# Gate and up products of a decoder layer's FFNs: pairs of column blocks by seven block products of sums instead of eight

## The chip, the cores and the metric

One core of one Trainium2 chip runs the kernel. The metric is the device time of one execution in microseconds (us). Engines are PE (TensorE; PEld is its weight load), DVE (VectorE), ACT (ScalarE), POOL (GpSimd) and SP (SyncE, which issues most DMAs).

## The reference

One layer of a decoder for 544 tokens (a prompt of 512 and 8 x 4 sampled ones) of width 1024, in float32: a SwiGLU FFN as a half step, a token mixer (gated DeltaNet and sliding-window attention) between an input and an output projection, and a second FFN. Each sub-layer is normalised before and after it, and shift, scale and gate come from a conditioning vector through `w_ada`. The change touches the two FFNs, D_FF is 2752:

```python
def swiglu(h, w_gate, w_up, w_down):
    return (jax.nn.silu(h @ w_gate) * (h @ w_up)) @ w_down

def decoder_layer(x, c, pos, conv_buf, S0, attend, p):
    mod = jax.nn.silu(c) @ p['w_ada'] + p['b_ada']
    ...
    h = rmsnorm(x, p['ffn1_norm_pre']) * (1 + sc1) + sh1
    x = x + 0.5 * g1 * rmsnorm(swiglu(h, p['ffn1_w_gate'], p['ffn1_w_up'], p['ffn1_w_down']), p['ffn1_norm_post'])
```

## The kernel before

The modulated input lies transposed in SBUF as a pair `hh`, `hl` of a rounded high part and its remainder, each 128 x 8 x 544: eight blocks of 128 input channels, and 544 tokens in two halves of TH = 272. Weights come in units of four blocks of 128 x 128. For a unit SP issues a DMA of 256 KB (`wload`), ACT casts it to the high part `hi` (L270), and DVE, in some units POOL, subtracts for the remainder `lo` (L271). PE then multiplies three terms per block, hi by xh, hi by xl and lo by xh, each for both token halves (`mm3`, L301): 24 matmuls of N = 272 to a unit.

An FFN goes in two halves of its inner width. In each, gate and up are computed for column blocks of 128 (`up`: two units each of gate and up, K = 1024), then `finish` takes silu of gate (ACT, L607), multiplies by up (DVE, L609) and splits the result into `fh`, `fl` (L612, L616); `last` does a mixed block of 64 and 64 columns; then `down` runs over eight output blocks and adds into `d`. The first half has column blocks 0 to 10, the second 0 to 9 and the mixed one. In the second FFN the first NFRONT = 5 blocks go one token half after the other, since the first half's tokens are ready sooner.

`Feed` holds the units in order. When unit i is to run, units up to i + 1 have been split and up to i + 2 been loaded (SPLIT_AHEAD, LOAD_AHEAD); four raw buffers and three of hi and lo (RAW_BUFS, HL_BUFS) bound it. Beside the feed, side streams run: `rest` computes the ada vectors of the later sub-layers during the first FFN, with 56 loads `wa` of 512 KB, each for four matmuls `adaps` (L467). The order of each engine is fixed when the kernel is built, by a planner that takes turns by the times that the streams yield; on the chip each engine works its own list in order.

Of the kernel before, what the change touches and what calls it, by code (L numbers as in the profile page):

```python
# [38 lines left out]
RAW_BUFS = 4  # L39
HL_BUFS = 3  # L40
# [152 lines left out]
class Unit:  # L193
# [3 lines left out]
    def __init__(self, parts, go, boxes=None, pool_lo=False, keep=None):  # L197

        self.parts, self.go, self.pool_lo, self.keep = parts, go, pool_lo, keep
        self.boxes = boxes or [p[:5] for p in parts or ()]  # L200


class Feed:


    def __init__(self, L):
        self.L, self.units, self.at, self.raws, self.ws = L, [], 0, {}, {}

# [8 lines left out]
    def prep(self, i):  # L217
        if i not in self.ws:
            self.fetch(i)
            u = self.units[i]  # L220
            dest = u.keep() if u.keep else None
            self.ws[i] = self.L.wsplit(self.raws.pop(i), u.boxes, u.pool_lo, dest) if u.parts else dest

    def run(self, upto=None):
        n = len(self.units) if upto is None else upto
        while self.at < n:
            i = self.at
            last = len(self.units) - 1
            for j in range(i, min(i + SPLIT_AHEAD, last) + 1):
                self.prep(j)  # L230
# [6 lines left out]
class Layer:  # L237
# [55 lines left out]
    def mm3(self, ps, w, kt, rows, x, kx, first, last, m=P, cs=(0, 1)):  # L293
# [5 lines left out]
        for i, (a, b, r) in enumerate(terms):  # L299
            for c in cs:  # L300
# [6 lines left out]
                )  # L307

# [74 lines left out]
    def setup(self):  # L383
# [202 lines left out]

    def ffn(self, pre, x, env, front, ndown, hook, each=None):
# [11 lines left out]
        def finish(gsrc, usrc, rows, j, shift, cs):  # L599
# [16 lines left out]
            nc.vector.tensor_tensor(out=fl[:rows, j, ts], in0=hf, in1=fh[:rows, j, ts].bitcast(F32), op=ALU.subtract)  # L616

# [37 lines left out]
        def down(half, b, cs):  # L655
# [3 lines left out]
            for k0 in (0, 4, 8):  # L659
                def go(w, k0=k0):  # L660
                    if k0 == 0:
# [30 lines left out]
        for half in range(2):  # L692
# [6 lines left out]
            for j in js:  # L699
                us += up(half, j, (0, 1))  # L700
# [1268 lines left out]
```

## Time and profile before

| | us |
|---|---|
| median of 3 runs (1605.84 to 1608.16) | 1606.75 |
| the profiled execution | 1608.77 |
| its span, first to last instruction | 1607.0 |
| mean granted TensorE clock in it | 0.983 |
| PE busy | 1537.5 |
| DVE busy | 887.6 |
| ACT busy | 640.1 |
| POOL busy | 305.9 |

The rows further down come from the profiled execution. Matmuls are pipelined: one lasts some 290 ns from start to end, and the next may start long before that end, so the distance of starts is the cost of one. The granted clock is a share of full speed.

### The profile page before, as it was taken

Reading aid. Unit: us, or ns where it says so; the run is one execution under the profiler, and the core shown is the slowest. Engines: PE = TensorE matmul, PEld = TensorE weight load, DVE = VectorE, ACT = ScalarE, POOL = GpSimd, SP = SyncE. Lnnn points to the kernel's source line nnn. Section 1 sums busy time; section 2 is a strip of 40 time slices with the busy share of each in tenths; the row PEclk is TensorE's granted clock in tenths of the full one; section 3 lists DMA queues with packets and bytes.
Section 4 is the critical chain, followed back from the end, with each engine's and each line's share of the span. In section 5 each row is a group of like instructions: output and inputs, shape, how many; then the busy total and the mean of one; then the engine's idle time right before and its main releaser. Section 6 shows DMA issues by size and latency. Waiting matters only on the chain.

```text
span 1607.0 us, 33057 instructions
## 1 busy us (share of the span) xinstructions
PE 1537.5 (96%) x12851; PEld 1418.5 (88%) x12851; DVE 887.6 (55%) x2384; ACT 640.1 (40%) x1449; POOL 305.9 (19%) x443
## 2 busy tenths in 40 slices
PE   7999999999998999998999999999979999999996
PEld 4799999999977999997778888889979999999995
DVE  5433322333598787688889568665474332233365
ACT  4322222222445544445575242223556332223363
POOL 2000000000343231231122134131458000000042
PEclk9999999999999999999999899999999999999998
DMA  9554445445655334653113243624515432333353
GB/s 314 169 183 138 153 136 159 147 148 153 190 167 178 100 75 107 165 135 77 45 45 80 77 121 83 167 55 130 158 53 158 115 86 87 94 87 89 83 152 111
DMA packets 316083, 199.69 MB, mean 124 GB/s; under 512 B 37508, under 2 KB 298335, under 8 KB 315638
## 3 DMA queue, kind: packets, MB, share of 16 engines
q1 hardware_dynamic: 315638, 197.46, 43.5%
q8 instruction: 101, 1.65, 0.4%
q14 instruction: 56, 0.46, 0.1%
q0 software_dynamic: 288, 0.11, 0.0%
HBM read 182.08 MB, written 16.36 MB: 123 GB/s over the span
## 4 chain that ended last, share of the span: by engine, by line
PE 77%; DVE 13%; ACT 3%; DMA 2%; issue 2%; POOL 2%; SPq 0%; DVEq 0%; ACTq 0%; POOLq 0%
PE pg L301 16%; PE pu L301 16%; PE pb L301 16%; PE pd L301 14%; PE adaps L467 3%; DVE y L1194 2%; DVE lo L271 2%; ACT hi L270 1%; PE pov L1065 1%; DVE X L1422 1%; PE pgu L301 1%; DVE s L1016 1%; PE psc L1012 1%; PE pkq L1281 1%; DVE xT L571 1%
## 5 line engine op out<-in xcount | busy, mean ns | idle before, releaser
L270 ACT CAST hi<-raw 128x512 fp32r<-128x512 f32 (+2 forms) x502 | 287.9, 581 | 613.1 <-PE pu L301 172.1
L271 DVE TENSOR_TENSOR lo<-raw,hi 128x512 fp32r<-128x512 f32 (+2 forms) x368 | 252.9, 688 | 385.8 <-ACT hi L270 378.7
L301 PE MATMUL pb<-hh,hi 128*128 128x272 f32 (+1 forms) x1008 | 234.9, 303 | 1.4 <-ACT hi L270 0.7
L271 POOL TENSOR_TENSOR lo<-raw,hi 128x512 fp32r<-128x512 f32 (+1 forms) x104 | 140.6, 1356 | 483.1 <-ACT hi L270 460.5
L301 PE MATMUL pb<-hh,lo 128*128 128x272 f32 (+1 forms) x1008 | 227.7, 296 | 1.3 <-POOL lo L271 0.7
L301 PE MATMUL pb<-hl,hi 128*128 128x272 f32 (+1 forms) x1008 | 227.2, 295 | 1.0 <-DVE hl L271 1.0
L301 PEld LDWEIGHTS pb<-hh,hi 128*128 128x128 f32 (+1 forms) x1008 | 164.6, 191 | 12.0 <-issue 6.5
L301 PE MATMUL pd<-fh,hi 128*128 128x272 f32 x704 | 171.3, 290 | 0.0
L301 PE MATMUL pd<-fl,hi 128*128 128x272 f32 x704 | 170.2, 289 | 0.0
L301 PEld LDWEIGHTS pb<-hl,hi 128*128 128x128 f32 (+1 forms) x1008 | 165.0, 190 | 3.6 <-DVE hl L271 1.5
L301 PEld LDWEIGHTS pb<-hh,lo 128*128 128x128 f32 (+1 forms) x1008 | 164.4, 191 | 4.1 <-DVE lo L271 1.4
L301 PE MATMUL pd<-fh,lo 128*128 128x272 f32 x672 | 162.4, 289 | 4.0 <-POOL lo L271 2.2
L301 PE MATMUL pg<-hh,hi 128*128 128x272 f32 x672 | 149.6, 292 | 7.5 <-ACT hh L538 3.6
L301 PE MATMUL pu<-hh,hi 128*128 128x272 f32 x672 | 148.2, 291 | 0.0
L301 PE MATMUL pg<-hl,hi 128*128 128x272 f32 x672 | 147.0, 289 | 0.3 <-DVE hl L539 0.2
L301 PE MATMUL pu<-hl,hi 128*128 128x272 f32 x672 | 146.1, 289 | 0.0
L301 PE MATMUL pu<-hh,lo 128*128 128x272 f32 x672 | 145.3, 288 | 0.7 <-POOL lo L271 0.7
L301 PE MATMUL pg<-hh,lo 128*128 128x272 f32 x672 | 145.6, 288 | 0.0
L301 PEld LDWEIGHTS pd<-fh,hi 128*128 128x128 f32 x704 | 119.9, 188 | 8.6 <-issue 4.2
L301 PEld LDWEIGHTS pg<-hh,hi 128*128 128x128 f32 x672 | 108.8, 189 | 19.6 <-ACT hh L550 5.0
L301 PEld LDWEIGHTS pd<-fl,hi 128*128 128x128 f32 x704 | 120.2, 188 | 0.0
L301 PEld LDWEIGHTS pd<-fh,lo 128*128 128x128 f32 x672 | 114.1, 188 | 5.6 <-POOL lo L271 2.9
(469 smaller groups left out, 2628.6 us busy)
## 6 DMA issues: line engine op xcount, KB each, us to landing
raw<-w_in SPq DMA_DIRECT2D x136, 256.0 KB, 3.2
wa<-w_ada SPq DMA_DIRECT2D x56, 512.0 KB, 4.4
raw<-ffn_w_gate SPq DMA_DIRECT2D x94, 256.0 KB, 2.9
raw<-ffn_w_up SPq DMA_DIRECT2D x94, 256.0 KB, 7.0
raw<-ffn_w_down SPq DMA_DIRECT2D x92, 256.0 KB, 3.0
wb<-w_ada SPq DMA_DIRECT2D x32, 256.0 KB, 5.8
S<-state_delta SPq DMA_DIRECT2D x8, 512.0 KB, 8.0
delta_sample<-S SPq DMA_DIRECT2D x8, 512.0 KB, 3.4
```

The lines of the kernel that those rows point to most:

```text
L270: self.nc.scalar.copy(out=hi, in_=raw)
L271: (eng or self.nc.vector).tensor_tensor(out=lo, in0=raw, in1=hi.bitcast(F32), op=ALU.subtract)
L301: self.nc.tensor.matmul(out=ps[:m, c, :TH], lhsT=a[:r, kt, :m], rhs=b[:r, kx, c * TH:(c + 1) * TH], start=first and i == 0, stop=last and ...
L467: self.ada_mm = nc.tensor.matmul(out=ps[32 * j:32 * j + 32, :], lhsT=self.cT[:, k, :], rhs=was[j], start=k == 0, stop=k == 7, skip_group_c ...
L571: nc.vector.tensor_tensor(out=self.xT[:, b, s], in0=self.xT[:, b, s], in1=t[:, :n], op=ALU.add)
L1012: nc.tensor.matmul(out=ps[:, i * 256:i * 256 + nk], lhsT=self.qT[64 * h:64 * h + 64, 2 * g + i, qb * P:(qb + 1) * P], rhs=self.kd[64 * h:6 ...
L1016: nc.vector.tensor_tensor_reduce(out=s[:, i, :nk], in0=ps[:, i * 256:i * 256 + nk], in1=am[:, lo:], scale=0.125, scalar=-3e38, op0=ALU.add ...
L1065: nc.tensor.matmul(out=po[64 * h:64 * h + 64, :256], lhsT=self.vn[:, c, 64 * g:64 * g + 64], rhs=pTs[kb][:, 2 * h:2 * h + 2, :], start=kb ...
L1194: nc.vector.scalar_tensor_tensor(out=y[:, :CVN], in0=cv[:, i:i + CVN], scalar=w[i], in1=y[:, :CVN], op0=ALU.mult, op1=ALU.add)
L1281: nc.tensor.matmul(out=pv[:, j], lhsT=kq[:, n, 0, c * P:(c + 1) * P], rhs=kq[:, n, :, c * P:(c + 1) * P], start=True, stop=True)
L1422: e.tensor_tensor(out=xs, in0=xs, in1=pv, op=ALU.subtract)
```

## The change

Two adjacent column blocks of gate (or up), two halves of K and two halves of the tokens make a product of 2 x 2 by 2 x 2 blocks, with eight block products. `quad` computes it with seven (12 matmuls each, by `mm3h`): four sums S1 to S4 of weight blocks, added on POOL, and four sums T1 to T4 of token blocks, made once per FFN by `token_sums` on DVE and ACT and kept as hi and lo. `pair` makes a gate quad and an up quad; the first block of an odd number stays with `up`, the second FFN's front blocks too. So there are 5 and 5 pairs in the two halves of the first FFN, 3 and 5 in the second: 36 quads. Each of the seven weight operands of a quad is split into hi and lo; before there were four.

The products 11 and 12 go to A and B, two banks of one PSUM tile, S3 and 22 to a third, D; after each product a step of `f1` to `f7` copies or adds between PSUM and two SBUF tiles `qlo` and `qhi`. Space for the token sums comes from `osw` of the mixer and from `xT` in the first FFN: `xT` is written to DRAM (`xsq`) at the start and loaded back by `close1`, called by the first `down` of the second half, which also waits until `rest` is done. Buffers: raw 6, hi and lo 4, sums 3, T_BUFS 5, V_BUFS 3; two wk PSUM banks instead of four while quads run. Quad units are split up to two units ahead. The vectors are loaded through ACT's queue, the constants `cst` at the mixer's start.

```diff
+    def mm3h(self, out, w, x, first):
+        hi, lo = w
+        xh, xl = x
+        for k in range(4):
+            for i, (a, b) in enumerate(((hi, xh), (hi, xl), (lo, xh))):
+                self.nc.tensor.matmul(out=out, lhsT=a[:, k, :], rhs=b[:, k, :], start=first and k == 0 and i == 0,
+                                      stop=k == 3 and i == 2, skip_group_check=True)
...
+    def token_sums(self, x, tiles, tmp):
...
+        def put(i, k, t):
+            th, tl = (tiles[i][n][:, k:k + 2, :] for n in range(2))
+            nc.scalar.copy(out=th, in_=t)
+            tt(out=tl, in0=t, in1=th.bitcast(F32), op=ALU.subtract)
...
+        for k in (0, 2):
+            t1, b = new("t1"), new("tb")
+            tt(out=t1, in0=f(hh, k, 0), in1=f(hh, k, 1), op=ALU.subtract)
+            tt(out=b, in0=f(hl, k, 0), in1=f(hl, k, 1), op=ALU.subtract)
+            tt(out=t1, in0=t1, in1=b, op=ALU.add)
+            put(0, k, t1)
...
+    def quad(self, name, w, c0, x, ts, ready, tmp, after_quad, begin, low, high):
...
+        def add(n, a, b, place=None):
+            raw[n] = raw[place] if place else self.ws.tile([P, 4, P], F32, tag="sum", name="sum")
+            with self.ahead(HP_S):
+                nc.gpsimd.tensor_tensor(out=raw[n], in0=raw[a], in1=raw[b], op=ALU.add)
...
+        def f1():
+            st["lo"] = tmp.tile([P, 2, TH], F32, tag="t", name="qlo", bufs=T_BUFS)
+            nc.scalar.copy(out=st["lo"][:, 0], in_=A())
+
+        def f2():
+            nc.vector.tensor_tensor(out=st["lo"][:, 0], in0=B(), in1=st["lo"][:, 0], op=plus)
+
+        def f3():
+            st["hi"] = tmp.tile([P, 2, TH], F32, tag="t", name="qhi", bufs=T_BUFS)
+            nc.scalar.copy(out=st["hi"][:, 0], in_=A())
+
+        def f4():
+            nc.scalar.copy(out=st["hi"][:, 1], in_=D())
+
+        def f5():
+            t = st["hi"][:, 1]
+            nc.vector.scalar_tensor_tensor(out=t, in0=A(), scalar=-1.0, in1=t, op0=mul, op1=sub)
...
+        plan = (("11", lambda: xb(0, 0), A, 1, f1), ("12", lambda: xb(1, 0), B, 1, f2), ("S2", ts[1], A, 0, f3),
+                ("S3", ts[2], D, 1, f4), ("S1", ts[0], A, 0, f5), ("22", ts[3], D, 0, f6),
+                ("S4", lambda: xb(1, 1), A, 0, f7))
...
+            def go(wt, i=i, xf=xf, out=out, first=first, after=after):
+                if i == 0:
+                    begin()
+                    st["ab"] = self.pj(name)
+                while i == 2 and not ready():
+                    yield 0.5
+                if i == 3:
+                    st["d"] = self.wd(name + "d")
+                yield from self.mm3h(out(), wt, xf(), bool(first))
+                after()
...
-            for j in js:
-                us += up(half, j, (0, 1))
+            if len(js) % 2:
+                us += up(half, js.pop(0), (0, 1))
+            for n, j in enumerate(js[::2]):
+                us += pair(half, j, n > 0)
...
+    def close1():
+        L.xT = xp.tile([P, 8, T], F32, tag="xT", name="xT")
+        nc.sync.dma_start(out=L.xT, in_=xsq)
+        while "ada" not in done:
+            yield 0.5
+        L.open_pw(4)
```

In the second FFN, on PE, at the end of one unit and the start of the next, the order before was:

```order
L301 MATMUL pg_18571<-hl_91,hi_18529 128x272 x2
L301 MATMUL pg_18571<-hh_90,lo_18530 128x272 x2
L301 MATMUL pu_18602<-hh_90,hi_18565 128x272 [waits DVE_49]
L301 MATMUL pu_18602<-hh_90,hi_18565 128x272
L301 MATMUL pu_18602<-hl_91,hi_18565 128x272 x2
```

On PE in a gate quad of the second FFN (hi_18257 is product 11 into A, hi_18323 is S3 into D, hi_18277 is 12 into B) it is now:

```order
L328 MATMUL pg_18308<-hl_94,hi_18257 128x272
L328 MATMUL pg_18308<-hh_93,lo_18258 128x272
L328 MATMUL pgd_18369<-t34_15971,hi_18323 128x272 [waits Activation_49]
L328 MATMUL pgd_18369<-t34_15971,hi_18323 128x272
L328 MATMUL pgd_18369<-t34_15971,lo_18324 128x272 [waits DVE_49]
...
L328 MATMUL pg_18308<-hh_93,hi_18277 128x272 [waits Activation_49]
L328 MATMUL pg_18308<-hl_94,hi_18277 128x272
```

The two units followed each other directly; now seven matmuls of S3 stand between 11 and 12, and 12 waits for ACT, which has A to copy.

On ACT at the same places, before (sil reads the finished gate, hi are casts of later units):

```order
L612 CAST fh_17545<-fhx_18561 128x544 [waits DVE_49]
...
L270 CAST hi_18693<-raw_18661 128x512 [waits DMAHW6_49,DVE_49,PE_49]
L607 ACTIVATE sil_18687<-pg_18571 128x544 [waits PE_49]
L270 CAST hi_18724<-raw_18697 128x512 [waits DMAHW7_49,DVE_49,PE_49]
L612 CAST fh_17545<-fhx_18689 128x544 [waits DVE_49]
```

On ACT in the quad now (L684 is f1, L694 is f4, L691 is f3):

```order
L283 CAST hi_18344<-sum_18186 128x512 [waits PE_49,Activation_49]
L798 CAST fh_18024<-qlo_18178 128x544 [waits DVE_49]
L684 COPY qlo_18321<-pg_18308 128x272 [waits PE_49]
L283 CAST hi_18365<-raw_18163 128x512 [waits DMAHW6_49,PE_49,Activation_49]
L694 COPY qhi_18363<-pgd_18369 128x272 [waits PE_49]
...
L283 CAST hi_18400<-raw_18282 128x512 [waits DMAHW0_49,PE_49]
L691 COPY qhi_18363<-pg_18308 128x272 [waits PE_49]
```

The copies out of PSUM, for which PE waits, stand behind casts for later units in ACT's list.

On DVE at the start of the first FFN, where the last block of x is modulated (L551) and block 0 is finished, before:

```order
L551 TENSOR_TENSOR hl_91<-ts_531,hh_90 128x32 [waits Activation_49]
L271 TENSOR_TENSOR lo_673<-raw_640,hi_672 128x512 [waits DMAHW4_49,PE_49,Activation_49]
L609 TENSOR_TENSOR fhx_668<-pu_581,sil_666 128x544 [waits PE_49,Activation_49]
L271 TENSOR_TENSOR lo_704<-raw_676,hi_703 128x512 [waits DMAHW5_49,Activation_49]
...
L609 TENSOR_TENSOR fhx_796<-pu_709,sil_794 128x544 [waits PE_49,Activation_49]
```

On DVE at that place now (t12 holds T1 and T2, t34 holds T3 and T4; L687 is f2 of the first gate quad):

```order
L575 TENSOR_TENSOR hl_94<-ts_529,hh_93 128x32 [waits Activation_49]
L640 TENSOR_TENSOR t4_701<-t4_701,hl_94 128x544 [waits DVE_49]
L284 TENSOR_TENSOR lo_713<-sum_636,hi_712 128x512 [waits PE_49,Activation_49]
...
L687 TENSOR_TENSOR qlo_731<-pg_718,qlo_731 128x272 [waits PE_49,Activation_49]
L630 TENSOR_TENSOR t1_761<-t1_761,tb_762 128x544 [waits DVE_49]
...
L623 TENSOR_TENSOR t12_545<-t2_768,t12_545 128x544 [waits Activation_49]
...
L623 TENSOR_TENSOR t34_546<-t3_794,t34_546 128x544 [waits Activation_49]
```

The token sums have come in around the splits; the last of T2 (t12) and of T3 (t34) stand behind the end of the first quad's second product.

On SP where the first FFN's second half goes over to `down`, before:

```order
L464 DMA wa_4265<-w_ada 128x1024 [waits PE_49]
...
L279 DMA raw_4167<-ffn1_w_down 128x4x128 [waits DMAHW0_49,DVE_49]
...
L464 DMA wa_4267<-w_ada 128x1024 [waits PE_49]
L464 DMA wa_4486<-w_ada 128x1024 [waits PE_49]
L279 DMA raw_4277<-ffn1_w_down 128x4x128 [waits DMAHW7_49,DMAHW6_49,DVE_49]
```

On SP there now (xT from xsq is the load of `close1`):

```order
L488 DMA wa_4522<-w_ada 128x1024 [waits DMAHW1_49,PE_49]
...
L2017 DMA xT_4520<-xsq_89 128x4352 [waits DMAHW7_49,PE_49]
...
L488 DMA wa_4524<-w_ada 128x1024 [waits DMAHW3_49,PE_49]
L488 DMA wa_4530<-w_ada 128x1024 [waits DMAHW4_49,PE_49]
...
L488 DMA wa_4580<-w_ada 128x1024 [waits DMAHW2_49,PE_49]
L292 DMA raw_4743<-ffn1_w_down 128x2x128 [waits DVE_49]
```

The loads for the ada products stood one or two at a time among the weights; now eleven stand in a row, behind the load of xT and ahead of the next weights.

## Rows read from the trace of the kernel before

**Rows 1.** the page: busy us (share) xinstructions of each engine; the chain's share by engine

```profile
PE 1537.5 (96%) x12851; PEld 1418.5 (88%) x12851; DVE 887.6 (55%) x2384; ACT 640.1 (40%) x1449; POOL 305.9 (19%) x443
...
PE 77%; DVE 13%; ACT 3%; DMA 2%; issue 2%; POOL 2%; SPq 0%; DVEq 0%; ACTq 0%; POOLq 0%
```

**Rows 2.** stretches: us, busy of PE, PEld, DVE, ACT, POOL; clock, DMA share, GB/s

```profile
80.00:400.00 320.00, 320.00 (x2525) 300.62 (x2524) 95.33 (x152) 89.07 (x150) 0.55 (x1) 1.00 0.51 153
...
440.00:480.00 40.00, 36.87 (x267) 32.11 (x265) 35.47 (x79) 19.72 (x48) 20.12 (x20) 1.00 0.58 168
480.00:520.00 40.00, 35.94 (x254) 31.20 (x251) 33.21 (x87) 18.88 (x44) 12.63 (x20) 0.96 0.61 180
...
900.00:1240.00 340.00, 323.71 (x3000) 299.27 (x2998) 213.35 (x617) 135.68 (x325) 126.29 (x133) 0.97 0.41 112
...
1240.00:1520.00 280.00, 280.00 (x2241) 280.00 (x2241) 90.53 (x134) 87.51 (x149) 9.39 (x8) 1.00 0.34 94
```

**Rows 3.** PE one by one in the second FFN: start us, us, engine, line, operation, xcount

```profile
1303.34 0.42 PE L301 MATMUL pu<-hh,hi 128*128 128x272 f32 x2
...
1306.34 0.42 PE L301 MATMUL pg<-hh,hi 128*128 128x272 f32 x2
...
1308.84 0.41 PE L301 MATMUL pg<-hl,hi 128*128 128x272 f32 x2
...
1309.34 0.42 PE L301 MATMUL pu<-hh,hi 128*128 128x272 f32 x2
```

**Rows 4.** ACT one by one there

```profile
1309.29 0.62 ACT L270 CAST hi<-raw 128x512 fp32r<-128x512 f32 x1 [2.33 <-PE pg L301]
1309.82 0.62 ACT L607 ACTIVATE sil<-pg 128x544 f32<-128x544 f32 x1
```

**Rows 5.** DVE one by one when the first FFN's block 0 ends

```profile
59.17 0.69 DVE L271 TENSOR_TENSOR lo<-raw,hi 128x512 fp32r<-128x512 f32 x1 [2.66 <-ACT hi L270]
59.78 0.72 DVE L609 TENSOR_TENSOR fhx<-pu,sil 128x544 f32<-128x544 f32 x1
60.41 0.68 DVE L271 TENSOR_TENSOR lo<-raw,hi 128x512 fp32r<-128x512 f32 x1
```

**Rows 6.** groups by form, whole span: out<-in shapes xcount | busy us, mean ns | idle before

```profile
L1883 ACT COPY dacc<-pb 128x272 f32<-128x272 f32 x12 | 4.6, 384 | 15.1 <-PE pb L301 15.1
...
L676 DVE TENSOR_TENSOR dacc<-pd,dacc 128x272 f32<-128x272 f32 x28 | 12.3, 438 | 26.6 <-PE pd L301 26.5
...
L271 POOL TENSOR_TENSOR lo<-raw,hi 128x512 fp32r<-128x512 f32 x103 | 140.3, 1366 | 478.8 <-ACT hi L270 456.3 <-DVE rms3a L344 11.3 <-PE ppt L1051 7.9
```

**Rows 7.** DVE's remainders by form, 1240 to 1520 us, then 900 to 1240 us

```profile
L271 DVE TENSOR_TENSOR lo<-raw,hi 128x512 fp32r<-128x512 f32 x84 | 58.0, 690 | 136.9 <-ACT hi L270 136.9
...
L271 DVE TENSOR_TENSOR lo<-raw,hi 128x512 fp32r<-128x512 f32 x30 | 21.8, 727 | 19.6 <-ACT hi L270 14.5 <-PE pkt L1301 3.2 <-PE prb L353 1.7
```

**Rows 8.** PE one by one around the ada products at the first FFN's start

```profile
55.31 1.05 PE L467 MATMUL adaps<-wa,cT 128*32 128x512 f32 x4
56.29 0.39 PE L301 MATMUL pg<-hh,hi 128*128 128x272 f32 x1
56.52 0.29 PE L301 MATMUL pg<-hl,hi 128*128 128x272 f32 x1
...
60.22 0.52 PE L301 MATMUL pg<-hh,hi 128*128 128x272 f32 x2
```

**Rows 9.** stretches at the first FFN's start, columns as in Rows 2

```profile
31.00:37.00 6.00, 6.00 (x21) 2.11 (x21) 5.65 (x24) 2.83 (x9) 0.00 (x0) 0.64 1.09 358
37.00:46.50 9.50, 9.50 (x53) 4.67 (x49) 0.71 (x2) 1.20 (x2) 0.00 (x0) 1.00 0.31 89
46.50:56.50 10.00, 7.63 (x47) 5.21 (x46) 9.47 (x36) 4.93 (x13) 0.00 (x0) 1.00 0.83 270
56.50:66.00 9.50, 9.50 (x70) 8.51 (x70) 3.35 (x6) 2.92 (x5) 0.00 (x0) 1.00 0.66 223
```

**Rows 10.** DMA issues on the page: out<-in, xcount, KB each, median us to landing

```profile
wa<-w_ada SPq DMA_DIRECT2D x56, 512.0 KB, 4.4
```

More of the change, by code (lines that the diff above doesn't have):

```diff
@@ L228, in run @@
             last = len(self.units) - 1
-            for j in range(i, min(i + SPLIT_AHEAD, last) + 1):
-                self.prep(j)
+            for j in range(i, min(i + 2, last) + 1):
+                if j <= i + SPLIT_AHEAD or self.units[j].src:
+                    self.prep(j)
+            for f in self.todo.pop(i, ()):
+                f()
             for j in range(i, min(i + LOAD_AHEAD, last) + 1):
@@ L660, in go @@
                 def go(w, k0=k0):
+                    if half and b == 0 and k0 == 0:
+                        yield from env["close"]()
                     if k0 == 0:
@@ L796, in open, with take, take_small @@
         self.mp = mp
[L797 removed]
+        self.win = self.a["w_in"][0]
+    def take(self):
+        self.osw = self.qT = self.mp.tile([P, 8, T], F32, tag="osw", name="osw")
+    def take_small(self):
+        mp = self.mq = self.L.pool("mq", 1, self.ctx)
+        self.L.cst = mp.tile([P, CST["n"]], F32, name="cst")
+        self.nc.sync.dma_start(out=self.L.cst, in_=self.a["c_cst"])
         self.kqs = mp.tile([P, NH, 2, NS], F32, name="kqs")
@@ L1807, in hook1, with tsums @@
         sch.spawn(L.boundary(sqd, env["d"], 2, 3, tmp, sqx, x, c, done), c)
-    env = {"tmp": tmp, "sqd": sqd}
+    def tsums(e, ta, tb):
+        e["ready"] = False
+        e["ts"] = [(t[:, i, 0], t[:, i, 1]) for t in (ta, tb) for i in range(2)]
+        yield from L.token_sums(x, e["ts"], e["tmp"])
+        e["ready"] = True
+    def close1():
+        L.xT = xp.tile([P, 8, T], F32, tag="xT", name="xT")
+        nc.sync.dma_start(out=L.xT, in_=xsq)
+        while "ada" not in done:
+            yield 0.5
+        L.open_pw(4)
+    env = {"tmp": tmp, "sqd": sqd, "close": close1}
     m1 = feed.add(L.ffn("ffn1", x, env, 0, NDOWN, hook1))
@@ L1856, in main @@
     def main():
+        nc.sync.dma_start(out=xsq, in_=L.xT)
+        ta = mx.mp.tile([P, 2, 2, 4, TH], F32R, tag="osw", name="t12")
+        tb = xp.tile([P, 2, 2, 4, TH], F32R, tag="xT", name="t34")
+        env["ready"] = False
+        sch.spawn(tsums(env, ta, tb), 0)
+        L.open_pw(2)
         sch.spawn(rest(), 2)
         yield from feed.run(m1)
+        mx.take()
         while not ({0, "ada"} <= done):
@@ L1938, in main @@
             yield from feed.run(feed.at + 1)
+        while sch.side:
+            yield from feed.run(feed.at + 1)
+        tb = xp2.tile([P, 2, 2, 4, TH], F32R, tag="xT", name="t34")
+        assert feed.at < len(feed.units) and not feed.units[feed.at].src
+        bufs["ready"] = False
+        sch.spawn(tsums(bufs, ta, tb), 0)
         yield from feed.run()
```

153 lines of the change are left out of this document (128 added, 25 removed).

## The prediction

> **What bounds the kernel now.** I read four views, from the whole to the detail. The page's busy line says that TensorE (PE) works 96% of the span and no other engine more than 55%, and its chain of waits gives PE 77% [rows 1]. The stretches show where those shares hold: between 80 and 400 us (the first FFN) and between 1240 and 1520 us (the second) PE is busy every microsecond, at a granted clock of 1.00, which is the upper of its two levels, 2.4 GHz; DVE is busy for 30 to 32% there and ACT for 28 to 31% [rows 2]. The instructions one by one show why nothing else ends last: the weight unit that starts at 1303.34 us is followed by the next at 1306.34 and the next at 1309.34, 24 matmuls in 3.00 us, 125 ns each, without a gap [rows 3]; the next weights' cast on ACT (0.62 us) and their remainder on DVE (0.69 us) take less than half of that [rows 4, 5]. So in the stretches that the change touches the number of matmuls is the time, as long as nobody makes PE wait. Outside them PE has idle time (4.1 of 40 us between 480 and 520) [rows 2]; the change does not touch that, except at the start.
>
> **The change, part by part.**
>
> *Matmuls removed.* A pair of column blocks takes, for gate and for up, eight products of 12 matmuls before and seven now. Pairs: 5 + 5 in the first FFN, 3 + 5 in the second, 18 in all, so 18 x 2 x 12 = 432 matmuls fewer, at 125 ns [rows 3]: **54.0 us off the path**. PE stays the engine with most to do: a pair takes 168 x 0.125 = 21.0 us of it. DVE has 14 remainders, 14 other operations on 272 or 544 columns: with the rows' spacing of about 0.62 us for the wide ones [rows 5] and 0.44 us for the narrow ones [rows 6] about 13.5 us; ACT 14 casts at 0.53 us from start to start [rows 4] and 14 copies and activations, about 12 us; POOL 8 additions of 128 x 512, which the trace shows only as a subtraction, 1.37 us each [rows 6], 11 us. So the new sums hide beside PE. What is not hidden is the order in which things become ready, which follows.
>
> *Turnarounds inside a quad (seven products).* Before, a PSUM tile was filled by 48 matmuls and read once. Now A and B lie in one tile, which the order treats as one thing: after product 11 ACT copies A before 12 may start, after 12 DVE adds B before S2 may start, and so on, four handovers per quad. The scheduler puts matmuls of the third tile (D) between as cover: 7 of them at the handovers to ACT, 5 at those to DVE, as the order of the change shows.
> At an ACT handover, counted from the start of the last matmul before it: this ends after 0.29 us. The matmul before it, the last reader of the weights' high part, has ended 0.125 us sooner, and that releases the next cast, which stands ahead of the copy in ACT's order; a cast began 0.04 us after such an end (pair of 1308.84 us, over at 1309.25; cast at 1309.29 us) [rows 3, 4]. So the cast starts at 0.20, the copy 0.53 us later [rows 4] at 0.73, takes 0.38 us (the copy out of PSUM of the same 272 columns) [rows 6] and with 0.04 us to PE the product may start at 1.15. The cover lasts 8 slots of 0.125 us, 1.00. Stall: 0.15 us.
> At a DVE handover: 0.29 + 0.04 + 0.44 (an addition out of PSUM on 272 columns) [rows 6] + 0.04 = 0.81 against 6 slots, 0.75. Stall: 0.06 us; where a remainder stands ahead on DVE, up to 0.6 us more [rows 5].
> A regular quad so loses 2 x 0.15 + 2 x 0.06 = 0.42 us. About a third of the quads are not regular: the order lets the next quad's first matmuls, or D's, in as cover, and their cast and remainder are then made just in time: 0.62 and 0.69 us in a row [rows 4, 5] against a unit of 1.5 us that cannot start them earlier than its own last matmul but one; such a quad loses 0.5 to 1 us more. I take 0.7 us as the mean. Remainders lasted 690 ns while POOL was nearly idle and 727 ns where it worked 126 of 340 us [rows 2, 7]; POOL will work half of the time here, so I add 0.05. 36 x 0.75 = **27 us back on the path**. Bounds: 0, if everything comes a little sooner; above, every handover restarts PE as badly as the matmul after the ada product at 56.29 us, which took 0.39 us and let its follower start 0.23 us later instead of 0.125 [rows 8], and every DVE handover finds a remainder in front: 0.42 + 4 x 0.1 + 2 x 0.6 = 2.0 us a quad, 72 us.
>
> *Token sums at the first FFN's start.* The quads need sums of x (T1 to T4), 28 DVE operations of 128 x 544. DVE is busy for 9.47 of the 10 us up to 56.5 us with modulating x, and then for only 3.35 of 9.5 [rows 9]; that idle time is what the sums can use. But by the order DVE has 22 wide operations after the last modulation up to the end of T2, and ten more up to T3, at 0.61 to 0.63 us [rows 5]: T2 at about 56.9 + 13.9 = 71 us, T3 at 77.3. Block 0 ends at about 60.2 us [rows 8] and the products 11 and 12 take 3.0 us: PE reaches S2 at 63.2 and waits 7.8 us, then S3 (72.5) and waits 4.8: 12.6 us. Where PE has been idle for 4 of 40 us the clock read 0.96 instead of 1.00 [rows 2]; half a microsecond for that: **13 us**. Bounds 6 (T3 covered by other work) and 18. x goes to DRAM and back because the sums take its place; the way out shares the queues with the first weights at a time when the DMAs have room (89 GB/s between 37 and 46.5 us, against 358 just before) [rows 9], so nothing for it.
>
> *The burst behind the first FFN's second half.* The first down block now waits until all of the ada products are done. By the order eleven loads of 512 KB stand behind the reload of x (2.2 MB) on SP, each waits for PE to release one of three buffers, and only some hundred matmuls of `down` lie between: 2.2 + 3 x 0.5 MB at 358 GB/s [rows 9] = 10.5 us until the first three are there, of which PE's own work covers 5 us; then a load's 4.4 us landing time [rows 10] over two buffers in flight, 2.2 us, meets 2.1 us of PE work (0.25 us for each of four ada matmuls [rows 8], nine of `down`). **7 us**; bounds 0 and 18. Queued behind these on SP are the weights of the next down blocks, so they can be no earlier.
>
> *The rest at nothing.* The sums before the second FFN's quads lie under its ten front units of a token half, where DVE is free for two thirds; without that cover they would cost what they cost at the start. The vectors are loaded by ACT's queue instead of POOL's, three buffers instead of four: at most 1 us at the start. Reopening PSUM pools and the later load of constants: below what can be seen.
>
> **Sum** against the profiled execution (span 1607.0, time 1608.8 us): -54 + 27 + 13 + 7 = -7 us, 1601.8. The profiled run lies 2.0 us above the median of 1606.75, so **1600 us** for the median. What a measurement of this kernel can tell from no change is about 0.2%, 3.2 us: faster means below 1603.5, slower above 1610.
>
> **A rule beside the rows.** In the stretch 440 to 480 us PE stood for 3.1 of 40 us and the clock stayed at 1.00 [rows 2]. The Trainium skill's page "TensorE: Matmul & The Clock Gate", section "A second HAM failure mode: psum-queue depth-cycling", says that short idles between groups of matmuls that cycle through PSUM banks let the clock swing between its two levels. The trace before does not show it, and it speaks against this change; it is the fourth rival below. Likewise the page "GPSIMD Engine Reference", section "Key points", says that POOL shares its SBUF interfaces with VectorE and contends with operations of two SBUF inputs, which all the remainders are; the rows above show 37 ns of it, and the fifth rival is what it would be in full.
>
> **The rivals.**
> 1. *The handovers are covered* (faster). For it: the cover misses by no more than 0.15 us, and ada matmuls lie between in the first FFN. Against: four handovers in each of 36 quads, each within a tenth of being late. At 0.2 us a quad (7 us), 10 at the start and 5 for the burst: -32, **1575 us**. Chance 0.24.
> 2. *The handovers miss by a chain* (slower): casts and remainders are queued ahead of the PSUM reads, so each late handover also delays the next cast, and the next unit comes late too. It decides above (54 - 20) / 36 = 0.94 us a quad. At 1.5 us: 54 us, **1627 us**. For it: ACT and DVE run in order, and half the units of a quad have their weights made within two units. Against: DVE at 65% has slack for two units. Chance 0.22.
> 3. *The start and the burst cost double* (40 us instead of 20): **1620 us**. For it: both are long waits of PE behind one queue; against: bounds of 18 each. Chance 0.07.
> 4. *The clock falls in the quads.* At 0.96, as in 480 to 520 us [rows 2], 36 quads of 11.2 us lose 16 us: **1616 us**. Chance 0.05.
> 5. *The change takes away no time*, because the products are no longer PE's alone: if POOL's additions kept DVE out altogether, DVE would need 13.5 + 11 = 24.5 us a pair, 0.5 more than PE's eight products took (192 x 0.125 = 24.0): 18 x 0.5 = 9 us lost, and 20 at the start and the burst: +29, **1636 us**. Rows show remainders 5% longer instead [rows 7]. Chance 0.02.
>
> **How the numbers follow.** Forecast (1590 to 1612 around 1600): 0.40. Of it 0.26 lie below 1603.5, 0.10 within 0.2%, 0.04 above. Rival 1 is faster; the others, 0.36, slower except for 0.04 that ends near no change. Faster 0.26 + 0.24 = 0.50, same 0.14, slower 0.36. The forecast's own range is 1590 to 1612; eight in ten needs rival 1's middle and rival 2's: 1572 to 1630.
>
> **What would show it.** Right: 432 matmuls fewer on lines that read 125 ns each; PE waits named after the copies (lines 684, 691) and DVE adds (687, 698) of 0.05 to 0.3 us each, some 130 of them, 25 us in sum; one gap of 12 us between 60 and 80 us that DVE's sums end; waits for wa loads of some 7 us near 420 us; clock 1.00 in the quads. Wrong: PE without gaps in the quads (rival 1), gaps that casts or remainders end and that add up to over 34 us (rival 2), or a clock below 1.00 there (rival 4).

## The result: 1701.7 us, 5.9% slower

| | before | changed |
|---|---|---|
| median, us | 1607.45 (4 runs) | 1701.67 (4 runs, 1698.37 to 1704.33) |
| profiled execution, us | 1608.77 | 1698.37 |
| mean granted clock | 0.983 | 0.961 |

The ratio is 1.0587 (95% interval 1.0565 to 1.0608). Forecast were 1600 us, with 1590 to 1612 as the forecast's own range and 1572 to 1630 as the range for eight cases in ten.

The page of the changed kernel, the line that answers to [rows 1]: busy us, share and instructions.

```profile
PE 1557.7 (92%) x12419; PEld 1400.2 (83%) x12419; DVE 1138.4 (67%) x2674; ACT 748.2 (44%) x1699; POOL 529.0 (31%) x578
```

PE has the 432 matmuls fewer (12851 to 12419), yet it counts 20 us more as busy, since slow restarts and time at the lower clock are busy time too. POOL has 223 us more, where 144 sums at 1.37 us [rows 6] make 197; DVE has 251 us more. Where it went is read by stages. First the kernel before: gate and up, then `down`, of the first FFN's first half; the same of its second half; then, behind the mixer, the same four of the second FFN. Each stretch goes from the first matmul of a stage to that of the next; the columns are those of [rows 2].

```profile
28.80:189.40 160.60, 158.23 (x1156) 137.22 (x1157) 59.70 (x129) 48.02 (x90) 0.00 (x0) 0.98 0.55 169
189.40:262.10 72.70, 72.70 (x574) 67.74 (x573) 17.54 (x32) 18.25 (x33) 0.00 (x0) 1.00 0.49 149
262.10:399.60 137.50, 137.50 (x1087) 128.61 (x1086) 43.50 (x70) 38.90 (x65) 0.55 (x1) 1.00 0.51 152
399.60:481.20 81.60, 77.70 (x578) 68.77 (x576) 59.47 (x118) 39.78 (x92) 35.27 (x33) 1.00 0.59 173
...
1179.30:1324.30 145.00, 139.52 (x1090) 137.74 (x1091) 67.84 (x120) 66.58 (x128) 53.74 (x43) 0.99 0.42 114
...
1390.40:1516.40 126.00, 126.00 (x1011) 126.00 (x1010) 42.61 (x62) 38.32 (x64) 0.55 (x1) 1.00 0.33 89
```

The same stages of the changed kernel:

```profile
30.50:221.30 190.80, 161.18 (x1044) 130.53 (x1045) 140.50 (x228) 79.73 (x161) 62.20 (x40) 0.95 0.49 157
221.30:292.30 71.00, 71.00 (x563) 67.06 (x562) 19.28 (x29) 19.09 (x34) 8.04 (x6) 1.00 0.48 146
292.30:439.80 147.50, 137.29 (x969) 117.57 (x968) 101.47 (x138) 67.37 (x132) 53.75 (x36) 0.99 0.49 148
439.80:528.80 89.00, 82.32 (x586) 69.47 (x584) 50.09 (x116) 38.14 (x88) 35.34 (x34) 0.99 0.65 186
...
1232.50:1400.80 168.30, 145.42 (x1021) 137.53 (x1019) 130.46 (x186) 85.97 (x173) 91.42 (x66) 0.93 0.35 95
...
1466.90:1604.80 137.90, 123.66 (x891) 116.49 (x889) 97.45 (x128) 65.55 (x130) 53.23 (x36) 0.98 0.31 82
```

Each of the four gate and up stages should have become shorter, by 3.0 us a pair: 160.6 to 145.6, 137.5 to 122.5, 145.0 to 136.0, 126.0 to 111.0. They became 190.8, 147.5, 168.3 and 137.9, which is 45, 25, 32 and 27 us too long. The second FFN's second half is the cleanest: ten quads and the mixed block, 26.9 us lost, 2.7 us a quad where the forecast had 0.75. Outside the four, the stage of the burst grew by 7.4 us, and some 7 us more are spread over the rest (5.6 in the mixer, 703.7 against 698.1 us), which the forecast put at nothing; no run took these apart.

In the stage of the ten quads the table of waits names (us in total, times, longest):

```profile
PE pgd L328 <- DVE lo L284: 10.3, 6, 2.7
PE pud L328 <- DVE lo L284: 2.3, 4, 1.0
PE pg L328 <- ACT hi L283: 0.9, 2, 0.5
PE pg L328 <- DVE qlo L687: 0.7, 2, 0.4
```

PE waits for remainders on DVE, by up to 2.7 us. The table has 14.2 of the 26.9 us. (Its last row shows what one tile for A and B does: S2 goes to A, and waits for L687, which adds B.) Some 3 us are the clock: in two stretches, each behind a stop of PE of over 2 us, it read 0.50, the lower level of 1.2 GHz, and matmuls started 0.23 us apart; after other stops of that length it did not fall. The first of them:

```profile
1497.20:1500.60 3.40, 3.40 (x17) 3.40 (x16) 2.56 (x6) 1.61 (x4) 0.00 (x0) 0.50 0.27 75
```

DVE's groups say why remainders are late: `lo` of a loaded block, then `lo` of a sum, mean 786 and 1201 ns; before, 690 [rows 7]. Below them stand the product with silu (L793, two SBUF operands), and a narrow addition out of PSUM (L687), which is as long as ever.

```profile
L284 DVE TENSOR_TENSOR lo<-raw,hi 128x512 fp32r<-128x512 f32 x357 | 279.2, 786 | 174.5 <-ACT hi L283 155.3 <-PE pgd L328 5.6 <-PE pu L328 2.5
L284 DVE TENSOR_TENSOR lo<-sum,hi 128x512 fp32r<-128x512 f32 x72 | 86.5, 1201 | 13.6 <-ACT hi L283 11.5
...
L793 DVE TENSOR_TENSOR qhi<-qhi 128x544 f32<-128x544 f32 x18 | 24.8, 1380 | 0.1
...
L687 DVE TENSOR_TENSOR qlo<-pg,qlo 128x272 f32<-128x272 f32 x18 | 7.8, 436 | 10.4 <-PE pg L328 10.3
```

POOL and then DVE one by one in a quad (start us, us):

```profile
1506.77 1.29 POOL L669 TENSOR_TENSOR sum<-raw 128x512 f32<-128x512 f32 x1 [0.70 <-DMA raw<-ffn_w_gate]
1508.14 1.72 POOL L669 TENSOR_TENSOR sum<-sum,raw 128x512 f32<-128x512 f32 x1
1509.82 1.73 POOL L669 TENSOR_TENSOR raw<-raw 128x512 f32<-128x512 f32 x1
```

```profile
1508.02 0.69 DVE L284 TENSOR_TENSOR lo<-raw,hi 128x512 fp32r<-128x512 f32 x1 [1.40 <-ACT hi L283]
1508.90 1.51 DVE L284 TENSOR_TENSOR lo<-sum,hi 128x512 fp32r<-128x512 f32 x1 [0.19 <-ACT hi L283]
1511.16 0.44 DVE L687 TENSOR_TENSOR qlo<-pu,qlo 128x272 f32<-128x272 f32 x1 [0.75 <-PE pu L328]
```

The remainder of 1508.90 starts while POOL's sum of 1508.14 runs (to 1509.86) and ends 0.55 us after it, as if it had only begun then. POOL's next sum starts at 1509.82, beside the rest of that remainder, and lasts 1.73 instead of 1.29 us. The addition at 1511.16, with one operand in PSUM, runs beside POOL in its normal 0.44 us. So a remainder and a sum take turns, and the one that starts second waits. Counted over this trace, 85 remainders of 128 x 512 start while a sum runs; they last 1.47 us in the mean, and 82 of them end 0.53 to 0.56 us after the sum. The 289 that meet no operation of POOL last 0.69 us, and so do the 31 that POOL joins when they already run.

### The profile page after: what moved, and what is told of

Read it like the earlier page. It is cut to its first block, busy times and chain, and to the rows that moved or that the text cites. A ratio compares the mean times of both kernels' runs of the same rounds, so it can differ in the third digit from the quotient of the medians.

```text
span 1696.6 us, 33229 instructions
## 1 busy us (share of the span) xinstructions
PE 1557.7 (92%) x12419; PEld 1400.2 (83%) x12419; DVE 1138.4 (67%) x2674; ACT 748.2 (44%) x1699; POOL 529.0 (31%) x578
## 5 line engine op out<-in xcount | busy, mean ns | idle before, releaser
L283 ACT CAST hi<-raw 128x512 fp32r<-128x512 f32 (+3 forms) x538 | 309.4, 584 | 498.3 <-issue 143.3
L284 DVE TENSOR_TENSOR lo<-raw,hi 128x512 fp32r<-128x512 f32 (+2 forms) x404 | 302.0, 751 | 265.3 <-ACT hi L283 246.0
L314 PE MATMUL pb<-hl,hi 128*128 128x272 f32 (+1 forms) x1008 | 230.8, 298 | 1.8 <-DVE hl L284 0.9
L669 POOL TENSOR_TENSOR raw<-sum,raw 128x512 f32<-128x512 f32 x36 | 47.7, 1324 | 262.5 <-DVE lo L284 251.1
L669 POOL TENSOR_TENSOR sum<-raw 128x512 f32<-128x512 f32 x36 | 56.5, 1571 | 179.1 <-DMA raw<-ffn_w_gate 152.6
L284 DVE TENSOR_TENSOR lo<-sum,hi 128x512 fp32r<-128x512 f32 x72 | 86.5, 1201 | 13.6 <-ACT hi L283 11.5
L328 PE MATMUL pg<-hh,hi 128*128 128x272 f32 x216 | 66.9, 310 | 7.1 <-ACT qlo L684 5.6
L328 PE MATMUL pg<-t,hi 128*128 128x272 f32 x288 | 60.6, 304 | 8.0 <-DVE qlo L687 4.2
L328 PE MATMUL pgd<-t,lo 128*128 128x272 f32 x144 | 44.8, 311 | 24.0 <-DVE lo L284 23.9
L328 PE MATMUL pgd<-t,hi 128*128 128x272 f32 x288 | 63.4, 301 | 3.2 <-ACT t L622 3.2
```

What stands on the lines that cost most here:

```text
L283: self.nc.scalar.copy(out=hi, in_=raw)
L284: (eng or self.nc.vector).tensor_tensor(out=lo, in0=raw, in1=hi.bitcast(F32), op=ALU.subtract)
L314: self.nc.tensor.matmul(out=ps[:m, c, :TH], lhsT=a[:r, kt, :m], rhs=b[:r, kx, c * TH:(c + 1) * TH], start=first and i == 0, stop=last and ...
L328: self.nc.tensor.matmul(out=out, lhsT=a[:, k, :], rhs=b[:, k, :], start=first and k == 0 and i == 0, stop=k == 3 and i == 2, skip_group_ch ...
L669: nc.gpsimd.tensor_tensor(out=raw[n], in0=raw[a], in1=raw[b], op=ALU.add)
```

## The experiments

Four runs took the changed kernel apart.

**Without POOL's sums.**

```diff
-            raw[n] = raw[place] if place else self.ws.tile([P, 4, P], F32, tag="sum", name="sum")
-            with self.ahead(HP_S):
-                nc.gpsimd.tensor_tensor(out=raw[n], in0=raw[a], in1=raw[b], op=ALU.add)
+            raw[n] = raw[place] if place else raw[a]
```

> POOL's 144 sums of weight blocks are left out (each sum operand is its first block, so the values differ from the reference). Theory A, POOL holds up DVE: in the changed kernel DVE's remainders last 688 ns with POOL idle and 1321 ns beside POOL. Without POOL's sums they should all be near 690 ns, and the quads lose at most the 27 us of turnarounds that the prediction had, instead of about 90: 1620 to 1645 us. Theory B, the turnarounds (copy, cast ahead of it, next product) cost 2.5 us a quad by themselves: the time stays above 1680 us.

Measured 1641.8 us (beside 1612.0 of the kernel before): 60 us less, theory A's number. Remainders last 697 ns. It does not get down to the time before, so A is not all.

**POOL's sums on DVE.**

```diff
-                nc.gpsimd.tensor_tensor(out=raw[n], in0=raw[a], in1=raw[b], op=ALU.add)
+                nc.vector.tensor_tensor(out=raw[n], in0=raw[a], in1=raw[b], op=ALU.add)
```

> The 144 sums move from POOL to DVE, everything else as in the changed kernel. Theory A: DVE has 144 x 0.62 = 89 us more to do (18.4 us of 21 a pair), yet no operation is held up: remainders near 690 ns, 1640 to 1670 us. Theory B: DVE is what the turnarounds wait for, so more work on it makes them worse: 1700 us or more.

Measured 1645.9 us: 56 us less with the same work on a fuller engine. DVE's groups are, in place of the two above:

```profile
L284 DVE TENSOR_TENSOR lo<-raw,hi 128x512 fp32r<-128x512 f32 x357 | 247.6, 700 | 146.9 <-ACT hi L283 134.8 <-PE poT L1537 1.7 <-PE pu L328 1.7
L284 DVE TENSOR_TENSOR lo<-sum,hi 128x512 fp32r<-128x512 f32 x72 | 49.4, 685 | 8.4 <-ACT hi L283 8.3
```

685 ns instead of 1201: the hold-up is POOL's, not that of a slower kind of tile. DVE as a whole is busy for 14 us less (1124.8 against 1138.4), with 144 operations more.

**The sums beside, unread.**

```diff
-            raw[n] = raw[place] if place else self.ws.tile([P, 4, P], F32, tag="sum", name="sum")
+            s = self.ws.tile([P, 4, P], F32, tag="sum", name="sum")
             with self.ahead(HP_S):
-                nc.gpsimd.tensor_tensor(out=raw[n], in0=raw[a], in1=raw[b], op=ALU.add)
+                nc.gpsimd.tensor_tensor(out=s, in0=raw[a], in1=raw[b], op=ALU.add)
+            raw[n] = raw[place] if place else raw[a]
```

> POOL makes the same 144 sums, but into a tile that nobody reads; the operands are as in e1_no_adds (values differ from the reference). Theory A: the sums do harm by running, not by being waited for: remainders beside POOL still last about 1.3 us and the time stays at 1685 to 1700 us. Rival C, the sums come too late for the casts (a chain of load, sum, sum, cast, remainder): as e1_no_adds, 1620 to 1645 us.

Measured 1680.0 us, 5 us below theory A's bound and far from rival C's. Of the 60 us that the sums cost, 38 are there although nobody reads them (1680.0 against 1641.8), and the other 22 come when they are read, and so waited for. Both have a part; the hold-up has the larger. The 80 remainders that start while such a sum runs last 1.36 us in the mean, as theory A had it; the mean of all is 825 ns:

```profile
L284 DVE TENSOR_TENSOR lo<-raw,hi 128x512 fp32r<-128x512 f32 x429 | 351.9, 825 | 205.4 <-ACT hi L283 189.3 <-PE pu L328 2.5 <-PE pgd L328 1.9
```

**The token sums left out.**

```diff
-        e["ts"] = [(t[:, i, 0], t[:, i, 1]) for t in (ta, tb) for i in range(2)]
-        yield from L.token_sums(x, e["ts"], e["tmp"])
+        e["ts"] = [tuple(t[:, k:k + 4, :TH] for t in x) for k in (0, 4, 0, 4)]
+        yield 0.0, 0.0
```

> The token sums T1 to T4 are left out in both FFNs (the quads read blocks of x in their place, values differ from the reference); the weight sums stay on POOL. The stages of the two traces put 20 us on the first FFN's start and 17 us on the second FFN's front blocks: if both are the token sums' doing, 1662 us; if only the start's (the prediction held the second FFN's to be hidden), 1680 us.

Measured 1665.1 us: 37 us less. The first FFN's first stage takes 168.8 us instead of 190.8, 22 less, and the second FFN's 154.3 instead of 168.3, 14 less. So the front blocks do not hide them. The two stages without the sums:

```profile
30.20:199.00 168.80, 153.50 (x1024) 127.44 (x1025) 116.73 (x194) 74.43 (x152) 59.64 (x40) 0.97 0.56 179
1211.90:1366.20 154.30, 141.13 (x1021) 134.75 (x1020) 101.06 (x159) 82.05 (x165) 88.88 (x66) 0.95 0.38 104
```

**A copy on POOL.** To see which work of POOL does it, against the kernel with the sums beside, unread:

```diff
-                nc.gpsimd.tensor_tensor(out=s, in0=raw[a], in1=raw[b], op=ALU.add)
+                nc.gpsimd.tensor_copy(out=s, in_=raw[a])
```

> As e3_adds_aside (POOL works beside, nobody reads its result, values differ from the reference), but POOL copies one block instead of adding two: 144 operations with one SBUF operand. e1_no_adds had 1642 us without them, e3_adds_aside 1680 us with the additions. If any POOL work beside DVE does the harm: 1665 to 1685 us, remainders beside POOL over 1 us. If only POOL operations with two SBUF inputs do it: 1640 to 1650 us, remainders near 690 ns.

Measured 1647.8 us, inside the second case: 6 us above the kernel without sums, which is about what two chips differ by (the kernel before took 1607.2 us beside this run and 1612.0 beside that one). POOL's copies, and all of DVE's remainders:

```profile
L669 POOL COPY sum<-raw 128x512 f32<-128x512 f32 x144 | 112.9, 824 | 478.4 <-DMA raw<-ffn_w_gate 302.2 <-DMA raw<-ffn_w_up 176.2
```

```profile
L284 DVE TENSOR_TENSOR lo<-raw,hi 128x512 fp32r<-128x512 f32 x429 | 308.5, 723 | 205.9 <-ACT hi L283 188.1 <-PE pu L328 2.5 <-PE pgd L328 1.7
```

The time and the mean of 723 ns speak for the second case, that two SBUF inputs are what matters; the single instructions do not. The mean is thinned out here as well: only 53 of the 429 remainders start while a copy runs. One copy on POOL, and the remainder on DVE that starts beside it:

```profile
1326.96 0.61 POOL L669 COPY sum<-raw 128x512 f32<-128x512 f32 x1 [9.02 <-DMA raw<-ffn_w_gate]
```

```profile
1327.15 0.97 DVE L284 TENSOR_TENSOR lo<-raw,hi 128x512 fp32r<-128x512 f32 x1
```

The remainder ends 0.55 us after the copy. So do 51 of the 53, at 0.53 to 0.56 us, just as 78 of the 80 beside the unread additions did. So of the two cases the time fits the second and what happens the first: a copy with its one operand holds a remainder up like an addition with two. It costs less because it is over sooner (0.61 us when alone, an addition 1.29): the remainders beside copies are 0.19 us late each, 10 us together; those beside additions 0.68 each, 54 us together. DVE's busy time on the pages rose in step, by 20 us with the copies and by 80 with the additions (1037.6 us without, 1057.1, 1117.9), and the kernel's time by 6 and 38.

**A and B in two PSUM tiles.** The turnarounds were the prediction's own main loss. The builder, which puts in the waits, goes by tiles; with two of them it no longer ties 12 to the copy of A. From here on each edit is shown against the run that its expectation starts from, this one against the sums on DVE and then against the changed kernel:

```diff
-        A, B, D = (lambda: st["ab"][:, 0, :TH]), (lambda: st["ab"][:, 1, :TH]), (lambda: st["d"][:, :TH])
+        A, B, D = (lambda: st["a"][:, 0, :TH]), (lambda: st["b"][:, 0, :TH]), (lambda: st["d"][:, :TH])
...
-                    st["ab"] = self.pj(name)
+                    st["a"] = self.pj(name)
+                if i == 1:
+                    st["b"] = self.pj(name + "b")
```

> As e2_adds_dve (1646 us), with A and B in two PSUM tiles, so that product 12 no longer waits for the copy of A, and S2 no longer for the addition of B; by the order every handover then has 12 matmuls, 1.5 us, of another product as cover. Theory T, what is left in the quads (about 1.3 us each in the second FFN's second half of e2_adds_dve) is the turnarounds: 25 to 40 us less, 1606 to 1621 us. Rival L, it is casts and remainders that come late: 1635 us or more.

> The changed kernel with A and B in two PSUM tiles alone; the weight sums stay on POOL. e6_ab_apart against e2_adds_dve put 28 us on the turnarounds, e2_adds_dve against the changed kernel 56 us on POOL's sums. If the two add up: 1672 us. If remainders that POOL holds up are the later of the two everywhere, the cover gains little: 1690 us or more. If the wider cover also hides the held-up remainders: 1650 us or less.

Measured 1617.4 us with the sums on DVE (ratio to before 1.0062, interval 1.0044 to 1.0081), inside theory T's bounds, and 1641.6 us with the sums on POOL. Of the second run's cases the third came: the wide cover alone gains 60 us, so it also hides most of what POOL holds up, and the two gains (56 and 60 us) make 84 together. The clean stage, 111.0 us of matmuls, in the four kernels:

| second FFN, second half, gate and up | one tile for A and B | two tiles |
|---|---|---|
| sums on POOL | 137.9 us | 121.1 us |
| sums on DVE | 124.4 us | 114.6 us |

Rows of the stretches: sums on DVE with one tile; sums on POOL with two; sums on DVE with two.

```profile
1429.00:1553.40 124.40, 120.01 (x891) 113.47 (x890) 91.94 (x161) 63.98 (x130) 0.55 (x1) 1.00 0.34 91
```

```profile
1428.10:1549.20 121.10, 113.93 (x891) 112.37 (x890) 98.81 (x128) 65.01 (x130) 52.24 (x36) 1.00 0.35 94
```

```profile
1408.00:1522.60 114.60, 114.03 (x891) 112.28 (x890) 93.02 (x161) 64.93 (x130) 0.55 (x1) 1.00 0.37 99
```

Without POOL's sums ten quads lose 13.4 us, 1.3 us each, of which the table of waits names 4.1 (casts 3.2, remainders 0.9); with two tiles it is 0.36 a quad, and the table names none. The clock is at its upper level, 2.4 GHz, in all three; in the changed kernel it read 0.98.

**Later first quads.** Two more plain blocks ahead of the quads in each FFN:

```diff
-            if len(js) % 2:
-                us += up(half, js.pop(0), (0, 1))
+            first = len(js) % 2 + (2 if half == 0 else 0)
+            for j in js[:first]:
+                us += up(half, j, (0, 1))
+            js = js[first:]
```

> As e6_ab_apart, with two more column blocks of each FFN's first half computed plainly ahead of the quads, so that the token sums have 24 us more to be made in; 2 pairs fewer, 6 us of matmuls more. e4_no_tsums put 37 us on the token sums. If they are hidden now, 20 to 30 us less than e6_ab_apart: 1580 to 1600 us, faster than before. If not (DVE is too full to take them), 0 to 6 us more than e6_ab_apart.

Measured 1613.2 us (ratio 1.0032, interval 1.0014 to 1.0050): outside both cases. The first stage came down as hoped, 166.8 to 155.5 us, but the first FFN's last `down` stage, with the wait for the ada products, grew from 89.3 to 96.0 us, and the second FFN's first stage went only from 157.5 to 156.0 us.

**Token sums after the front, and no wait for the ada products.**

```diff
+        if feed.at < mo + 8 * NFRONT:
+            yield from feed.run(mo + 8 * NFRONT)
         tb = xp2.tile([P, 2, 2, 4, TH], F32R, tag="xT", name="t34")
```

> As e7_ab_late, with the second FFN's token sums begun only when its ten front units of a token half are done. In e7_ab_late that stage loses 30 us of PE, before it lost 13; POOL works there (it makes remainders) and DVE's sums have two SBUF operands. If the sums beside POOL are the cause: 12 to 17 us less, 1596 to 1602 us. If the sums simply lack DVE time, the loss moves behind the front: 1610 to 1615 us.

```diff
-        while "ada" not in done:
-            yield 0.5
-        L.open_pw(4)
+        return
+        yield 0.0
...
+        L.open_pw(4)
```

> As e8_front, without the wait for the ada products at the first down block of the first FFN's second half (the PSUM pool is widened only after that FFN). Prediction's term for this burst: 7 us; in e7_ab_late the stage loses 7 to 10 us more than before, but its waits for wa loads read 4.3 us only. If the wait is the cause: 4 to 8 us less than e8_front. If it is the boundary behind it: no change within 2 us.

The first: 1613.4 us, no change. The stage still takes 154.8 us; PE now waits 5.4 us for the last token sum behind the front, as the second case had it. The second: 1594.4 us (ratio 0.9917, interval 0.9896 to 0.9938), 19 us less where 4 to 8 were expected. This kernel has no wait, and it widens the PSUM pool later; the two are not told apart. The stage of the wait, first in this kernel, then in the one with the wait:

```profile
384.00:461.70 77.70, 76.31 (x587) 68.48 (x585) 50.37 (x115) 39.23 (x90) 35.23 (x33) 1.00 0.72 213
```

```profile
385.40:482.90 97.50, 87.98 (x600) 71.73 (x596) 52.17 (x117) 37.93 (x89) 35.24 (x34) 0.97 0.67 192
```

19.8 us, all of the difference, are in this stage. The waits named for wa loads in the kernel with the wait are 4.0 us in all. By the distance of starts its 510 matmuls of `down` take 76.9 us, and without the wait 67.4, and its 56 ada matmuls 15.9 us, without it 48 of them 7.7; why they are slower was not taken apart. Without the wait the stage is also 3.9 us shorter than in the kernel before (81.6 us), and no run tells whether that kernel could gain these without quads.

**No quads in the second FFN's first half.**

```diff
+            if half == 0 and front:
+                first = len(js)
```

> As e9_no_burst, without the two pairs that the second FFN's first half still had: its six blocks behind the front are plain, so the token sums have 72 us until the first quad. 48 matmuls more, 6.0 us. In e9_no_burst this stage takes 154.5 us, 126.0 us of it matmuls, before 145.0 us with 132.0 us of matmuls. If what it loses beyond before (15 us) is the wait for the token sums and the sums beside POOL: 1583 to 1589 us. If it is only the wait of 5 us that the trace names: 1594 to 1597 us.

Measured 1587.5 us (ratio 0.9872, interval 0.9855 to 0.9888), inside the first case. The stage takes 151.6 instead of 154.5 us:

```profile
1165.70:1317.30 151.60, 142.52 (x1090) 140.07 (x1091) 89.90 (x149) 71.07 (x136) 52.78 (x42) 0.97 0.40 109
```

That is 3 us of the 7, with 6.0 us more of matmuls in it: beyond its matmuls the stage now loses 19.6 us, 28.5 in the run that it starts from and 13.0 in the kernel before. The other 4 lie outside it and within the spread of the runs (the profiled execution, 1592.68 us, is the slowest of four). It is the fastest of all kernels here, 1.3% under the kernel before, with 14 of the 18 pairs.

## Why the prediction was wrong

**The gain was right.** 432 matmuls went, and where no one waits a matmul still costs 125 ns: in the two-tile kernel 888 of them, 111.0 us, take 114.6 us.

**The term that failed is the quads': 27 us forecast, some 93 measured** (36 quads at 2.6 us: 25 and 27 us in the two stages that make no token sums; in the other two what is left after 22 and 14 us of token sums, 23 and 18 us; lower clocks are in it, some 3 us in the last stage). It failed in two steps.

The first step is "I add 0.05" for POOL, drawn from 690 and 727 ns. Both are means over stretches in which most remainders met no POOL operation [rows 7], so they thinned out the effect: of the 30 behind the 727 ns three began while POOL was at work, and these lasted 0.94 to 1.28 us. The same trace shows it elsewhere too: in the kernel before, the second FFN's front, where POOL makes remainders, has two operations of DVE of the same size:

```profile
L616 DVE TENSOR_TENSOR fl<-fhx,fh 128x272 fp32r<-128x272 f32 x10 | 9.0, 901 | 3.2 <-ACT fh L612 3.1
```

```profile
L609 DVE TENSOR_TENSOR fhx<-pu,sil 128x272 f32<-128x272 f32 x10 | 4.4, 440 | 18.9 <-PE pu L301 18.7 <-ACT sil L607 0.2
```

`fl` reads two SBUF tiles and takes twice as long in the mean (five of the ten last 1.2 to 1.3 us) as `fhx`, which reads one of its operands from PSUM. The fifth rival was this mechanism, at a chance of 0.02, and its price was reckoned wrongly too, as a sum of busy times. DVE is busy for only 67% of the span [the page's line above]; what hurts is that a sum's remainder comes 0.5 us later in the mean, in a chain whose handovers the forecast itself put within 0.15 us of their cover. The Trainium skill's page "GPSIMD Engine Reference", section "Key points", names DVE instructions with two SBUF inputs as ones that contend with POOL; the runs agree (1201 against 685 ns). I had cited it and let the mean overrule it.

The second step is the turnaround itself: 0.42 us in a regular quad, 0.7 as a mean, measured 1.3 us without POOL. The arithmetic of when a product may start was close; a late start costs more than its lateness. The restart that I kept for the upper bound (0.39 us and a follower 0.23 us later) [rows 8] is the rule: in the kernel with the sums on DVE and one tile, 42 starts in the last gate and up stage are late, and the median follower comes 0.23 us behind. PE in the changed kernel before S1, which waits for ACT's copy of A:

```profile
1541.04 0.29 PE L328 MATMUL pud<-t,hi 128*128 128x272 f32 x1
1541.32 0.52 PE L328 MATMUL pu<-t,hi 128*128 128x272 f32 x2
1541.67 0.29 PE L328 MATMUL pu<-t,lo 128*128 128x272 f32 x1
```

S1 starts 0.28 us after the last matmul of the cover instead of 0.125: 0.15 us late, as reckoned. The two matmuls of the second line then take 0.35 us from start to start instead of 0.25, and these 0.10 us the sum did not have. Before S4, at a handover of DVE that the table of waits does not list either:

```profile
1505.43 0.28 PE L328 MATMUL pu<-hl,hi 128*128 128x272 f32 x1
1505.62 0.40 PE L328 MATMUL pg<-hh,hi 128*128 128x272 f32 x1
1505.85 0.29 PE L328 MATMUL pg<-hl,hi 128*128 128x272 f32 x1
1505.98 0.29 PE L328 MATMUL pg<-hh,lo 128*128 128x272 f32 x1
```

The starts lie 0.19 and 0.23 us apart instead of 0.125 each: 0.17 us lost, 0.07 of it lateness (0.06 reckoned), and all of it looks busy. In a quad without a late cast or remainder three handovers show so (S2 is 0.14 us late), some 0.7 us where the regular quad had 0.42. In the kernel with the sums on DVE and one tile PE is busy for 120.0 of 124.4 us with 111.0 us of work at full clock, so two thirds of its 13.4 us look busy.

**Token sums: 13 at the start forecast, 22 measured; 0 in the second FFN forecast, 14 measured.** PE stands at the places foreseen, before S2 (`pg`) and S3 (`pgd`), between 60 and 90 us:

```profile
PE pgd L328 <- ACT t L622: 3.2, 1, 3.2
PE pg L328 <- ACT t L622: 2.8, 1, 2.8
...
PE pg L328 <- DVE t L623: 1.0, 1, 1.0
```

That is 7.0 us of named waits, less than the 12.6 reckoned; the stage as a whole loses more than these, and how the 22 us divide was not measured. The cover named for the second FFN, "DVE is free for two thirds", was a wrong reading: under the front units DVE is busy for 45.0 of 74.7 us in the kernel before, and in the changed kernel for 76.9 of 92.5:

```profile
1179.30:1254.00 74.70, 69.22 (x528) 67.44 (x529) 45.00 (x87) 45.88 (x93) 53.74 (x43) 0.98 0.51 135
```

```profile
1232.50:1325.00 92.50, 76.75 (x531) 73.32 (x530) 76.88 (x116) 49.80 (x102) 60.98 (x46) 0.90 0.40 106
```

POOL makes remainders in this stretch, too, but that the sums beside POOL are the cause is not shown: made behind the front they cost as much (1613.4 us).

**The burst: 7 us forecast; in the changed kernel that stage is 89.0 instead of 81.6 us, 7.4 more.** The mechanism was only partly the one given: waits for wa loads come to 1.5 us there. Part of the growth is ada work moved in from earlier stages (44 ada matmuls instead of 39). So that the number came out is in part luck; in the faster kernels the same wait cost 19 us.

**The rivals.** The second, a chain of late handovers, is what was left without POOL's sums (1.3 us a quad, where it had 1.5); in the changed kernel the fifth's mechanism came on top, which it did not have. The fourth, the clock, had a part: in the changed kernel it reads 0.93 in the second FFN's first stage and 0.98 in the second (0.99 and 1.00 before), so at 168 x 0.06 + 138 x 0.02 it is at most some 13 us there, and 191 x 0.03, some 6 us, in the first FFN's first stage (0.95, before 0.98); these means count time in which PE stood, too. In the clean stage it is back at 1.00 as soon as POOL's sums or the shared tile are gone, so there it follows the waits. The range ended at the second rival's 1627 us, and the bound of 2.0 us a quad had no term for POOL.

## What to carry to other kernels

Before work is given to POOL because it is idle, look for DVE operations with two SBUF operands beside it, and take their duration where an operation of POOL is really under way, not a mean over a stretch, which hides it; the longer POOL's single operations, the later DVE's; the cost is the delay of the chain, even where both engines are far from full. An accumulation tile that is read between products needs a whole product of another tile as cover, and two accumulators in one tile are one where waits go by tiles. A scheme that saves PE work can pay only where its preparation has a place to hide: here the same idea with sums on DVE, separate tiles, plain blocks first and no forced wait turned 5.9% slower into 1.3% faster, some 20 us of the 42 us of matmuls that 14 pairs save.

## What the runs showed of the hardware that I had not expected

- POOL and DVE take turns when DVE's operation has two SBUF operands (float32, 128 x 512): a remainder that starts while POOL adds or copies ends 0.53 to 0.56 us after it (82 of 85 and 78 of 80 beside additions, 51 of 53 beside copies); 0.69 us became up to 1.8. A sum in its turn took 1.73 instead of 1.29 us. With one operand in PSUM DVE is not held up (0.44 us).
- PE that starts 0.065 us late loses 0.17 us, and the views count it as busy.
